# First stage of a two-layer trunk: four receptance buffers, three key-pair buffers, adaLN steps between the mixes with their copies on ScalarE

## The chip, the cores and the metric

The kernel runs as one program on one core of one Trainium2 chip. The metric is the device time of one execution in microseconds (us), of the whole kernel from the first to the last instruction with what lies around it. Engines are named as in the profile: PE is TensorE's matrix multiplication, PEld its weight load, DVE VectorE, ACT ScalarE, POOL GpSimd, SP SyncE (which issues DMAs here). "ACTq" and "SPq" are the queues of ACT and SP on which DMAs are issued.

## What is computed

A trunk of two layers works on 256 latent tokens and 256 context tokens of width 1024, in float32. Each sub-layer is modulated by shift, scale and gate vectors that come from a small product with the layer's adaLN weights. Layer 0 mixes tokens with a bidirectional RWKV-7 recurrence and ends with a SwiGLU; layer 1 has a pooling mixer and a mixture of 8 experts. Cut to what the change touches:

```
mod   = silu(c) @ ada_w[i] + ada_b[i]          # and the same from c_ctx for the context tokens
sh1, sc1, gt1, sh2, sc2, gt2 = split(mod, 6)
h     = x * (1 + sc1) + sh1                    # and hc from ctx
xx    = shifted(h) - h
xr, xw, xk, xv, xa, xg = (h + xx * mu[m] for m in range(6))
r = xr @ w_rkv[0];  k = xk @ w_rkv[1];  v = xv @ w_rkv[2]
d_lora = tanh(xw @ w1) @ w2;   a = sigmoid(a0 + (xa @ a1) @ a2)
kk = k * k_k / |k * k_k|  per head
# wkv7 scan over time in both directions, gate, output product, layer_norm, SwiGLU; then layer 1
```

## The kernel before, in words

The order of instructions on each engine is fixed when the program is built: a scheduler goes through the source and lists the instructions of each engine by when it expects their operands and buffers, so the order on an engine can differ from that of the source. Later, from the recurrence on, a list scheduler of its own with a table of work items decides. Everything named here is the first stage, which comes ahead of the recurrence.

**adaLN steps.** The adaLN product of one layer and one of its six vectors is cut into four steps of `ada_step` (L311). A step loads 1 MB of `ada_w` into one of the raw buffers (L316; `hvr`, `wr` and the two halves of `hvw` for the first eight steps, then `hvr` and `wr`) and issues 16 matmuls (`ada_mm`, L255) into one PSUM bank that all steps share (`ADAB`, pb_68 in the rows of the order). After every fourth step the bank is copied into the tile `ab` (`ada_copy`, L259), two transposes turn it (`ada_turn`, L263), and `ada_put` (L267) adds it to the vectors in `small`. For two of the vectors `ada_store` (L270) writes 1024 single values to `mod_d` in DRAM. The first eight steps give scale and shift, without which no mix can be modulated; eight more stand one behind each pair of the key and of the receptance stage.

**Mixes.** `mixed` (L353) makes the six mixes x + xx * mu before modulation: xk, xw, xa on DVE (L359, 24 instructions of 128x512), xg, xr and xv "beside", scaled on ACT (L356) and added on POOL (L357). Then `modulated` applies scale and shift (`affine`: L388 and L394 on DVE, L391 on ACT) and corrects the edges of the grid (L330).

**Key stage** (L472). Weights come in pairs of output tiles: `wtile` loads 1 MB into a raw buffer, `split_w` splits it into a high part on ACT (L442, two halves) and a low part (L443, the first half on DVE, the second on POOL), each tile takes 24 matmuls (L237) of 128x512. Of each tile the product is copied to `kt` (L480) and squared (L482) on ACT; a matmul sums over heads (L484), DVE takes the reciprocal (L486, L487) and multiplies (L488), and a DMA on ACT's queue writes kt to DRAM (L489). kt has two buffers.

**Receptance stage** (L505). The same for r, with 256 columns; ACT copies the product to `rt` (L514), which has one buffer, and issues its DMA (L515) to `k_d`.

**Into the recurrence.** Then the early pools close. SP reads the first keys back (L1186) and loads the lora weights (L1187, `arena<-in_lr`); ACT issues the next adaLN loads (L702) and splits the lora weights (`lrsh`, L1191; `lrsl` on DVE, L1194); PE multiplies with them (L747), and the recurrence begins.

Of the kernel before, what the change touches and what calls it, by code (L numbers as in the profile page):

```python
# [8 lines left out]
F32 = mybir.dt.float32  # L9
F32R = mybir.dt.float32r  # L10
I32 = mybir.dt.int32
AF = mybir.ActivationFunctionType
# [5 lines left out]
P = 128  # L18
D = 1024
DT = 8  # L20
NT = 512
# [77 lines left out]
class Sched:  # L99


    LAT = {("DVE", "DVE"): 0.06, ("ACT", "ACT"): 0.06, ("POOL", "POOL"): 0.05, ("PE", "PE"): 0.0, ("ACT", "DVE"): 0.12,
           ("PE", "ACT"): 0.14}
# [24 lines left out]
    def order(self):  # L128
# [3 lines left out]
        while cand:  # L132
# [36 lines left out]
            for n in o.next:  # L169
                n.wait -= 1  # L170
                n.ready = max(n.ready, fin + (0.0 if o.nbytes else self.LAT.get((o.eng, n.eng), self.LAT_ELSE)))
                if n.wait == 0:
# [28 lines left out]
def kernel(ctx: ExitStack, tc: tile.TileContext, I: dict, out: bass.AP, dbg=None):  # L201
    nc = tc.nc
# [22 lines left out]
    def C(n, a=0, b=None):  # L225
        o, w = CONST[n]
        return consts[:, o + a:o + (w if b is None else b)]
# [3 lines left out]
    def V(n, dt):  # L231
        return vec[:, n, dt:dt + 1]

    def mm3(ps, a, b, start, stop, pin=None):

        for n, (x, y) in enumerate(((0, 0), (0, 1), (1, 0))):
            i = nc.tensor.matmul(ps, lhsT=a[x], rhs=b[y], start=start and n == 0, stop=stop and n == 2)  # L237
            if pin:
                pin(i)
# [8 lines left out]
    ab = cst.tile([P, 256], F32, name="ab")  # L248
# [4 lines left out]
    def ada_mm(ps, w, k, h):  # L253
        for g in range(2):
            nc.tensor.matmul(ps[64 * h + 32 * g:64 * h + 32 * g + 32, 0:256], lhsT=sct[:, k], rhs=w[:, 256 * g:256 * g + 256],  # L255
                             start=(k == 0), stop=(k == DT - 1))

    def ada_copy(ps):
        nc.vector.tensor_copy(ab, ps[:, 0:256])  # L259

    def ada_turn(pt):
        for j in range(2):
            nc.tensor.transpose(pt[:, P * j:P * j + P], ab[:, P * j:P * j + P], ident)  # L263

    def ada_put(l, w, pt):
        m = mods[l][:, 8 * w:8 * w + 8].rearrange("p (g j) r -> p g j r", g=4)
        nc.vector.tensor_tensor(m, m, pt[:, 0:256].rearrange("p (j g r) -> p g j r", j=2, g=4)[:, :, :, 0:2], op=ALU.add)  # L267

    def ada_store(l, w):
        nc.sync.dma_start(mod_d[l, w // 3].rearrange("(d p) -> p d", p=P), mods[l][:, 8 * w:8 * w + 8, 0])  # L270
# [6 lines left out]
    ADAB = PB[5]  # L277
# [13 lines left out]
    kq = es_e.enter_context(tc.tile_pool(name="kq", bufs=2))  # L291
# [4 lines left out]
    def raw(shape):  # L296

        i = raw_at[0] % (4 if raw_at[0] < 8 else 2)
        raw_at[0] += 1
        return raw_b[i].rearrange("p (a b) -> p a b", a=shape)  # L300

    def xtile(name, dt=F32):
        return xs_p.tile([P, DT, NT], dt, tag="x", name=name)
# [7 lines left out]
    def ada_step():  # L311

        (n, k2) = ada_at
        l, w = todo[n]
        wt = raw(2)
        nc.sync.dma_start(wt, I["ada_w"][l, w, 2 * k2:2 * k2 + 2].rearrange("k p n -> p k n"))  # L316
        for j in range(2):
            for h in range(2):
                ada_mm(ADAB, wt[:, j, 512 * h:512 * h + 512], 2 * k2 + j, h)
        if k2 == 3:  # L320
            ada_copy(ADAB)
            pt = gen()
            ada_turn(pt)
            ada_put(l, w, pt)
            if w % 3 == 2:
                ada_store(l, w)
        ada_at[:] = [n + 1, 0] if k2 == 3 else [n, k2 + 1]
# [25 lines left out]
    def mixed(m, t, sl=slice(0, 512), beside=False):  # L353
        for dt in range(DT):
            if beside:
                nc.scalar.activation(t[:, dt], xx[:, dt, sl], AF.Copy, scale=V(V_MU + m, dt))  # L356
                nc.gpsimd.tensor_tensor(t[:, dt], t[:, dt], xcT[:, dt, sl], op=ALU.add)  # L357
                continue
            nc.vector.scalar_tensor_tensor(t[:, dt], xx[:, dt, sl], V(V_MU + m, dt), xcT[:, dt, sl],  # L359
                                           op0=ALU.mult, op1=ALU.add)  # L360
        return t

    LAT = slice(256, 512)
    xk = mixed(2, xtile("xk"))
    xw = mixed(1, xtile("xw"))
    xa = mixed(4, xtile("xa"))
    xgr = xtile("xgr").rearrange("p a (b c) -> p b a c", b=2)
    xg, xr = mixed(5, xgr[:, 0], LAT, True), mixed(0, xgr[:, 1], LAT, True)
    mixed(3, xv, beside=True)

    for _ in range(8):
        ada_step()
    hvw = hv.tile([P, 4, 4, 256], F32R, tag="hvw", name="hvw1")
    wsp_b = [[hvw[:, 2 * i + j] for j in range(2)] for i in range(2)]
    lr1 = early.tile([P, DT, 384], F32, name="lr1")
# [40 lines left out]
    def modulated(m, x, on=None, then=None, t=None):  # L416
        t = x if t is None else t
        for h in range(2):
            for dt in range(4 * h, 4 * h + 4):
                affine(m, x, t, dt, on)  # L420
            edges(m, t, h)
            for dt in range(4 * h, 4 * h + 4):
                if then:
                    then(t, dt)
# [7 lines left out]
    def lora(xm, o, n):  # L432
        ps = gen()
        for k in range(DT):
            nc.tensor.matmul(ps[:, 0:n], lhsT=lr1[:, k, o:o + P], rhs=xm[:, k], start=(k == 0), stop=(k == DT - 1))
        return ps

    def split_w(w):
        r = []
        for h in range(2):  # L440
            hi, lo = wsp_b[h]
            nc.scalar.activation(hi, w[:, 4 * h:4 * h + 4], AF.Copy)  # L442
            (nc.vector, nc.gpsimd)[h].tensor_tensor(lo, w[:, 4 * h:4 * h + 4], hi, op=ALU.subtract)  # L443
            r.append((hi, lo))
        return r
# [3 lines left out]
    modulated(2, xk, None, split_x(xks, [nc.vector]))  # L449
    modulated(4, xa, nc.scalar)  # L450
    ps = lora(xw, 0, 512)
    tl = kq.tile([P, 2, NT], F32, tag="kt", name="tl")
    nc.scalar.activation(tl[:, 0], ps, AF.Tanh)
    ps = lora(xa, P, 512)
    nc.scalar.activation(tl[:, 1], ps, AF.Copy)
# [11 lines left out]
    def wtile(m, dp):  # L467
        w = raw(DT)
        nc.sync.dma_start(w, I["w_rkv"][m, dp])
        return w  # L470

    for dp in range(4):  # L472
        ws = split_w(wtile(1, dp))
        for j in range(2):
            dt = 2 * dp + j
            ps = gen()
            for k in range(DT):
                mm3(ps, [v[:, k % 4, P * j:P * j + P] for v in ws[k // 4]], [v[:, k] for v in xks], k == 0, k == DT - 1)
            kt = kq.tile([P, 2, NT], F32, name="kt")
            nc.scalar.activation(kt[:, 0], ps, AF.Copy)  # L480
            sq = kq.tile([P, NT], F32, name="sq", bufs=1)
            nc.scalar.activation(sq, ps, AF.Square, scale=V(V_KK, dt))  # L482
            pn = gen()
            nc.tensor.matmul(pn, lhsT=C("bones"), rhs=sq)  # L484
            rec = kq.tile([P, NT], F32, name="rec", bufs=1)
            nc.vector.tensor_scalar(rec, pn, 1e-24, None, op0=ALU.max)  # L486
            nc.vector.reciprocal(rec, rec)  # L487
            nc.vector.scalar_tensor_tensor(kt[:, 1], kt[:, 0], kkh[:, dt:dt + 1], rec, op0=ALU.mult, op1=ALU.mult)  # L488
            nc.scalar.dma_start(k_d[dt, :, 0:1024], kt)  # L489
        ada_step()  # L490
        if dp == 0:
            modulated(5, xg)
            ps = lora(xg, 256, 256)
            nc.scalar.activation(sgg, ps[:, 0:256], AF.Tanh, scale=0.5)
            nc.vector.tensor_scalar(sgg, sgg, 0.5, 0.5, op0=ALU.mult, op1=ALU.add)
            xrt = xtile("xrs", F32R).rearrange("p a (b c) -> p b a c", b=2)
            xrs = [xrt[:, 0], xrt[:, 1]]
            modulated(0, xr, None, split_x(xrs, [nc.gpsimd]))
        if dp == 1:
            xvm = xtile("xvm")  # L500
            modulated(3, xv, None, None, xvm)
            xvs = [xvh, hv.tile([P, DT, NT], F32R, tag="hvl", name="xvl")]
            for dt in range(DT):
                split_x(xvs, [nc.gpsimd, nc.vector])(xvm, dt)
    for dp in range(4):  # L505
        ws = split_w(wtile(0, dp))
        for j in range(2):
            dt = 2 * dp + j
            ps = gen()
            for k in range(DT):  # L510
                mm3(ps[:, 0:256], [v[:, k % 4, P * j:P * j + P] for v in ws[k // 4]], [v[:, k] for v in xrs],
                    k == 0, k == DT - 1)
            rt = kq.tile([P, 256], F32, name="rt", bufs=1)
            nc.scalar.activation(rt, ps[:, 0:256], AF.Copy)  # L514
            nc.scalar.dma_start(k_d[dt, :, 1024:1280], rt)  # L515
        ada_step()
# [807 lines left out]
    p_a, _ = affine(0, 1, 1, None, "pa")  # L1324
# [740 lines left out]
```

## Time and profile before

| | |
|---|---|
| time of the kernel before | 1380.35 us, median of 3 runs (1375.9 to 1383.91) |
| the profiled execution | 1385.43 us, span in the trace 1383.6 us |
| mean granted TensorE clock in it | 0.891 |
| busy: PE, DVE, ACT, POOL | 84%, 66%, 43%, 22% of the span |
| DMA | 287.94 MB, 208 GB/s over the span |

A row of the timeline gives start, busy time, engine, line, operation, output<-inputs with shapes and count, and in brackets how long the engine sat idle before it and what released it. Several like instructions are merged into one row, so its time is from the first start to the last end. A stage's row gives for each engine its busy time and number of instructions.

### The profile page before, as it was taken

To read this page: it belongs to the slowest core of one execution; us is meant where nothing else is said; L and a number is where in the kernel's file an instruction comes from. 1 tells how busy PE (TensorE), PEld (TensorE's weight loads), DVE (VectorE), ACT (ScalarE), POOL (GpSimd) and SP (SyncE) were. 2 spreads that over 40 slices of the span, in tenths; PEclk is the share of its full clock that TensorE was granted. 3 is DMA by queue.
4 is the path that set the end of the run, shared out by engine and by line. 5 is a ranking of instruction groups with operands and counts; after the bars stand their busy time and mean duration, and the time that the engine had idled before them with its cause. 6 is when DMAs were issued, how large, how long until landed. Compare 5 with 4: busy or idle time off the path is not lost. (4 is left out here: it accounts for less than half of the span.)

```text
span 1383.6 us, 26439 instructions
## 1 busy us (share of the span) xinstructions
PE 1165.1 (84%) x10345; PEld 884.2 (64%) x10345; DVE 913.4 (66%) x1792; ACT 596.7 (43%) x1222; POOL 305.8 (22%) x403
## 2 busy tenths in 40 slices
PE   1589658998788787869979999995997999987996
PEld 0256447975556565645569898985785865665673
DVE  7797516868957868234587768675697955723774
ACT  3342116375544563312234444532585844511660
POOL 6341110027530063520162224014000000000000
PEclk8599788998769997788989999997998999999898
DMA  9225545545556374656944554564997844589980
GB/s 363 92 91 196 160 171 172 189 121 163 152 132 172 64 186 117 162 125 192 369 154 146 181 190 155 197 260 178 420 420 287 327 135 164 179 331 414 417 345 32
DMA packets 131546, 287.94 MB, mean 208 GB/s; under 512 B 63536, under 2 KB 90288, under 8 KB 108208
## 3 DMA queue, kind: packets, MB, share of 16 engines
q1 hardware_dynamic: 120000, 249.14, 51.6%
q10 hardware_dynamic: 11376, 36.67, 8.0%
q8 instruction: 90, 1.47, 0.5%
q14 instruction: 80, 0.66, 0.2%
HBM read 273.17 MB, written 12.60 MB: 207 GB/s over the span
## 5 line engine op out<-in xcount | busy, mean ns | idle before, releaser
L1270 DVE TENSOR_TENSOR wl<-arena,wh 128x512 fp32r<-128x512 f32 x266 | 214.9, 833 | 90.2 <-ACT wh L1269 77.6
L1269 ACT ACTIVATE wh<-arena 128x512 fp32r<-128x512 f32 x266 | 162.4, 628 | 134.8 <-PE pb L237 117.8
L237 PE MATMUL pb<-usl,wh 128*128 128x256 f32 x352 | 102.9, 293 | 10.0 <-DVE usl L1419 10.0
L237 PE MATMUL pb<-ush,wl 128*128 128x256 f32 x352 | 102.0, 290 | 1.7 <-DVE wl L1270 1.7
L237 PE MATMUL pb<-ush,wh 128*128 128x256 f32 x352 | 101.4, 291 | 1.8 <-DVE fsg L1437 1.8
L1270 DVE TENSOR_TENSOR wl<-slot,wh 128x512 fp32r<-128x512 f32 x130 | 85.0, 687 | 21.4 <-ACT wh L1269 21.2
L1269 ACT ACTIVATE wh<-slot 128x512 fp32r<-128x512 f32 x130 | 79.3, 629 | 43.5 <-PE pb L237 28.8
L1060 ACT ACTIVATE sv<-pb 64x128 f32<-64x128 f32 x128 | 34.6, 271 | 116.2 <-PE pb L1054 92.6
L237 PEld LDWEIGHTS pb<-usl,wh 128*128 128x128 f32 x352 | 69.9, 199 | 13.7 <-DVE usl L1419 11.0
L1081 DVE TENSOR_TENSOR sv<-pb,wc 64x128 f32<-64x128 f32 x112 | 32.2, 288 | 69.8 <-PE pb L1071 29.2
L237 PE MATMUL pb<-wh,xsh 128*128 128x512 f32 (+1 forms) x192 | 74.2, 392 | 3.1 <-DVE x L1713 3.1
L1643 POOL TENSOR_SCALAR oh<-consts,consts 128x128 f32<-128x128 f32 x14 | 9.8, 710 | 298.3 <-PE pb L237 246.6
L1301 POOL TENSOR_TENSOR arena<-arena,rows 128x2048 f32<-128x2048 f32 x11 | 51.5, 4686 | 108.4 <-DMA arena<-in_ffn_w_dram 108.4
L237 PE MATMUL pb<-wl,xsh 128*128 128x512 f32 (+1 forms) x192 | 75.0, 390 | 0.0
L237 PE MATMUL pb<-wh,xsl 128*128 128x512 f32 (+1 forms) x192 | 72.2, 376 | 0.0
L237 PEld LDWEIGHTS pb<-ush,wl 128*128 128x128 f32 x352 | 69.9, 199 | 3.4 <-DVE wl L1270 2.0
L237 PEld LDWEIGHTS pb<-ush,wh 128*128 128x128 f32 x352 | 69.1, 198 | 4.2 <-DVE fsg L1437 2.0
L930 POOL TENSOR_TENSOR arena<-arena,X 128x126 f32<-128x126 f32 (+22 forms) x124 | 60.1, 485 | 38.5 <-DMA X<-s 29.4
L932 POOL TENSOR_TENSOR arena<-arena 128x126 f32<-128x126 f32 (+22 forms) x124 | 55.3, 446 | 9.7
L1711 PE MATMUL pb<-yf,consts 128*128 128x512 f32 x72 | 42.1, 724 | 17.6 <-issue 14.7
L842 PE MATMUL pb<-arena 64*64 64x192 f32 x512 | 49.0, 339 | 3.2 <-DVE GA L857 1.9
L237 PE MATMUL pb<-hvw,xvh 128*128 128x256 f32 x256 | 47.3, 286 | 1.4 <-DVE hvw L663 1.0
(440 smaller groups left out, 2996.3 us busy)
## 6 DMA issues: line engine op xcount, KB each, us to landing
slot<-in_moe_w_dram SPq DMA_DIRECT2D x62, 1024.0 KB, 13.6
arena<-in_moe_w_dram SPq DMA_DIRECT2D x58, 1024.0 KB, 14.0
arena<-in_ffn_w_dram SPq DMA_DIRECT2D x33, 1024.0 KB, 5.2
arena<-in_ada_w_dram ACTq DMA_DIRECT2D x28, 512.0 KB, 5.2
ada<-in_ada_w_dram ACTq DMA_DIRECT2D x28, 512.0 KB, 4.7
hvr<-in_w_rkv_dram SPq DMA_DIRECT2D x12, 1024.0 KB, 5.3
wr<-in_ada_w_dram SPq DMA_DIRECT2D x10, 1024.0 KB, 8.9
sv<-v_d SPq DMA_DIRECT2D x128, 64.0 KB, 3.6
```

The lines of the kernel that those rows point to most:

```text
L237: i = nc.tensor.matmul(ps, lhsT=a[x], rhs=b[y], start=start and n == 0, stop=stop and n == 2)
L842: nc.tensor.matmul(pb(g)[hs, 192 * j:192 * j + 192], lhsT=kap_b[kap.i][hs, c + j], rhs=kbi_b[kbi.i][hs, c + j])
L930: eng.tensor_tensor(mv, T[:, cs, j:j + 1].to_broadcast([P, nci, nii]), X[:, ii, j].unsqueeze(1).to_broadcast([P, nci, nii]), op=ALU.mult)
L932: eng.tensor_tensor(T[:, cs, ii], T[:, cs, ii], mv, op=ALU.subtract)
L1060: nc.scalar.activation(sv_(si, d, 1)[zd(d)], bank[zd(d), 0:128], AF.Copy, scale=-1.0)
L1081: nc.vector.tensor_tensor(sv_(si + 1, d, 0)[zd(d)].rearrange("p (h x) -> p h x", h=2), bank[zd(d), 128:256].rearrange("p (h x) -> p h x", ...
L1269: nc.scalar.activation(hi, r[:, o:o + PART], AF.Copy)
L1270: nc.vector.tensor_tensor(lo, r[:, o:o + PART], hi, op=ALU.subtract)
L1301: S.behind(nc.gpsimd.tensor_tensor(w, w, gt.unsqueeze(1).to_broadcast(w.shape), op=ALU.mult))
L1643: eng.tensor_scalar(oh[:, t], C2("iota", P * b, P * b + P), posm[:, t, e:e + 1], None, op0=ALU.is_equal)
L1711: nc.tensor.matmul(ps, lhsT=ohT[:, t], rhs=yf[:, 512 * j:512 * j + 512], start=True, stop=True)
```

## The change

It edits the first stage at four places. The adaLN copy can be put on ScalarE, and in the first stage it is (in the recurrence it stays on VectorE). The first eight adaLN steps are written between the mixes, four behind xk and four behind xw, where they stood behind all six. The pool of key pairs gives `kt` (and `tl`, which has the same tag) three buffers for two, and `rt` four for one.

```diff
-    def ada_copy(ps):
-        nc.vector.tensor_copy(ab, ps[:, 0:256])
+    def ada_copy(ps, on=None):
+        if on is nc.scalar:
+            nc.scalar.activation(ab, ps[:, 0:256], AF.Copy)
+        else:
+            nc.vector.tensor_copy(ab, ps[:, 0:256])
...
         if k2 == 3:
-            ada_copy(ADAB)
+            ada_copy(ADAB, nc.scalar)
...
     xk = mixed(2, xtile("xk"))
+    for _ in range(4):
+        ada_step()
     xw = mixed(1, xtile("xw"))
+    for _ in range(4):
+        ada_step()
     xa = mixed(4, xtile("xa"))
...
-    for _ in range(8):
-        ada_step()
...
-    tl = kq.tile([P, 2, NT], F32, tag="kt", name="tl")
+    KT = 3
+    tl = kq.tile([P, 2, NT], F32, tag="kt", name="tl", bufs=KT)
...
-            kt = kq.tile([P, 2, NT], F32, name="kt")
+            kt = kq.tile([P, 2, NT], F32, name="kt", bufs=KT)
...
-            rt = kq.tile([P, 256], F32, name="rt", bufs=1)
+            rt = kq.tile([P, 256], F32, name="rt", bufs=4)
```

Since the scheduler lists each engine's instructions anew, the order on the engines moves too. On ACT, at the front of the program, right behind the mixes (xgr is the tile of xg and xr, hvw the split weights, xkh the high part of xk). Before:

```order
L356 ACTIVATE xgr<-xx,small 128x256 x16
L391 ACTIVATE xw<-xw,small 128x256 x8
L391 ACTIVATE xa<-xa,small 128x256 x8
L442 ACTIVATE hvw_284<-hvr 128x1024 x2
L428 ACTIVATE xkh<-xk 128x512 x8
```

With the change:

```order
L359 ACTIVATE xgr<-xx,small 128x256 x16
L260 ACTIVATE ab<-pb_68 128x256 x2
L448 ACTIVATE hvw_284<-hvr 128x1024 x2
L397 ACTIVATE xw<-xw,small 128x256 x8
L397 ACTIVATE xa<-xa,small 128x256 x8
L434 ACTIVATE xkh<-xk 128x512 x8
```

Both copies of `ab` stand right behind the scaled mixes, and the high halves of the first weight pair stand ahead of the modulation of xw and xa instead of behind it. On DVE at the same place the two copies are gone from between the last mix and the first modulation. Before:

```order
L359 SCALAR_TENSOR_TENSOR xa<-xx,small,xcT 128x512 x8
L259 COPY ab<-pb_68 128x256
L267 TENSOR_TENSOR small<-small,pb_63 128x16
L378 TENSOR_SCALAR small<-small 128x16
L259 COPY ab<-pb_68 128x256
L267 TENSOR_TENSOR small<-small,pb_64 128x16
L381 TENSOR_TENSOR musc<-small 128x48 x2
L388 TENSOR_SCALAR xw<-xw,small 128x256 x8
```

With the change:

```order
L362 SCALAR_TENSOR_TENSOR xa<-xx,small,xcT 128x512 x8
L270 TENSOR_TENSOR small<-small,pb_63 128x16
L384 TENSOR_SCALAR small<-small 128x16
L270 TENSOR_TENSOR small<-small,pb_64 128x16
L387 TENSOR_TENSOR musc<-small 128x48 x2
L394 TENSOR_SCALAR xw<-xw,small 128x256 x8
```

All of DVE's mixes still stand ahead of the first `ada_put`. On PE in the receptance stage (pb_68<-wr is an adaLN step, xrs the two parts of xr, pb_70<-sq and pb_67<-sq the last sums of the key stage), before:

```order
L237 MATMUL pb_65<-xrs,hvw_284 128x256 x10
L255 MATMUL pb_68<-wr,sct 32x256 x8
L484 MATMUL pb_70<-sq,consts 128x512
L237 MATMUL pb_66<-xrs,hvw_284 128x256 x2
L237 MATMUL pb_67<-xrs,hvw_284 128x256 x2
L255 MATMUL pb_68<-wr,sct 32x256 x8
L237 MATMUL pb_66<-xrs,hvw_284 128x256 x22
L237 MATMUL pb_67<-xrs,hvw_284 128x256 x22
L255 MATMUL pb_68<-wr,sct 32x256 x8
L237 MATMUL pb_69<-xrs,hvw_284 128x256 x2
```

With the change:

```order
L491 MATMUL pb_70<-sq,consts 128x512
L237 MATMUL pb_64<-xrs,hvw_284 128x256 x10
L237 MATMUL pb_65<-xrs,hvw_284 128x256 x10
L255 MATMUL pb_68<-wr,sct 32x256 x8
L237 MATMUL pb_66<-xrs,hvw_284 128x256 x2
L237 MATMUL pb_67<-xrs,hvw_284 128x256 x2
L237 MATMUL pb_66<-xrs,hvw_284 128x256 x12
L237 MATMUL pb_67<-xrs,hvw_284 128x256 x12
L237 MATMUL pb_66<-xrs,hvw_284 128x256 x10
L237 MATMUL pb_67<-xrs,hvw_284 128x256 x10
L255 MATMUL pb_68<-wr,sct 32x256 x8
L237 MATMUL pb_69<-xrs,hvw_284 128x256 x2
```

The key stage's last sum no longer stands behind an adaLN step, and the second step has moved from the start of the second pair to its end (the third, likewise, from the start of the third pair to its end). SP's order is the same in both.

## Rows read from the trace of the kernel before

**Rows 1.** Busy time of the engines by stretch of the span: the front's mixes, the first modulation, the lora and first key products. Columns: stretch, its length, busy time and count of PE, PEld, DVE, ACT, POOL, granted PE clock, DMA share, GB/s.

```profile
36.00:46.00 10.00, 0.00 (x0) 0.00 (x0) 10.00 (x11) 0.00 (x0) 7.82 (x7) 0.50 0.00 1
56.00:66.00 10.00, 7.45 (x23) 3.04 (x24) 10.00 (x36) 10.00 (x19) 1.32 (x1) 0.50 0.33 112
66.00:90.00 24.00, 24.00 (x91) 14.24 (x91) 23.94 (x59) 11.05 (x23) 7.37 (x9) 1.00 0.25 88
```

**Rows 2.** The waits between 140 and 212 us, the receptance stage and the way into the recurrence: engine, line, released by, total us, times, longest.

```profile
ACT rt L514 <- DMA k_d<-rt: 19.3, 4, 8.0
...
PE pb L255 <- DMA wr<-in_ada_w_dram: 13.1, 3, 8.0
```

**Rows 3.** The timeline of DVE from the last mix on.

```profile
38.64 7.71 DVE L359 SCALAR_TENSOR_TENSOR xa<-xx,small,xcT 128x512 f32<-128x512 f32 x8
...
53.58 0.42 DVE L259 COPY ab<-pb 128x256 f32<-128x256 f32 x1 [5.73 <-PE pb L255]
54.53 0.17 DVE L267 TENSOR_TENSOR small<-small,pb 128x16 f32<-128x16 f32 x1 [0.53 <-PE pb L263]
54.74 0.33 DVE L381 TENSOR_TENSOR musc<-small 128x48 f32<-128x48 f32 x2
54.98 2.67 DVE L388 TENSOR_SCALAR xw<-xw,small 128x256 f32<-128x256 f32 x8
...
64.96 2.33 DVE L330 TENSOR_TENSOR xa<-xa,musc 128x8 f32<-128x8 f32 x1
```

**Rows 4.** The timeline of PE at the front: the first adaLN group's last step, the first transposes, the end of the second group, the first lora product.

```profile
19.75 1.07 PE L255 MATMUL pb<-hvw,sct 128*32 128x256 f32 x16 [0.97 <-DMA hvw<-in_ada_w_dram]
...
46.74 0.69 PE L263 MATMUL pb<-consts,ab 128*128 128x128 f32 x2 [25.92 <-DVE ab L259]
...
50.78 2.72 PE L255 MATMUL pb<-hvw,sct 128*32 128x256 f32 x32
...
60.48 6.88 PE L435 MATMUL pb<-xw,lr 128*128 128x512 f32 x9 [1.37 <-ACT xa L391]
```

**Rows 5.** The timeline of ACT at the front.

```profile
17.32 6.48 ACT L356 ACTIVATE xgr<-xx,small 128x256 f32<-128x256 f32 x16
...
54.74 4.04 ACT L391 ACTIVATE xw<-xw,small 128x256 f32<-128x256 f32 x8 [30.94 <-DVE small L267]
...
62.61 1.99 ACT L442 ACTIVATE hvw<-hvr 128x1024 fp32r<-128x1024 f32 x2
```

**Rows 6.** The DMA throughput between 10 and 40 us, in 40 slices of 0.75 us: the adaLN loads of the first eight steps.

```profile
DMA  9999999999999998899999999999993000000000
```

**Rows 7.** The timeline of POOL at the front: its last adds, and the first low half of a weight.

```profile
37.01 6.81 POOL L357 TENSOR_TENSOR xgr<-xgr,xcT 128x256 f32<-128x256 f32 x6
64.68 2.58 POOL L443 TENSOR_TENSOR hvw<-hvr,hvw 128x1024 fp32r<-128x1024 f32 x1 [20.86 <-ACT hvw L442]
```

**Rows 8.** The timeline of PE in the key stage, at its only gap there.

```profile
99.70 0.82 PE L237 MATMUL pb<-xkh,hvw 128*128 128x512 f32 x2 [3.77 <-DVE hvw L443]
```

**Rows 9.** The timeline of PE at the end of the receptance stage and behind it.

```profile
188.91 5.53 PE L237 MATMUL pb<-xrs,hvw 128*128 128x256 f32 x44 [0.52 <-DVE hvw L443]
208.21 1.08 PE L255 MATMUL pb<-arena,sct 128*32 128x256 f32 x8 [13.76 <-DMA arena<-in_ada_w_dram]
```

**Rows 10.** The timeline of POOL in the same stretch: the low halves of the last three receptance pairs.

```profile
164.08 2.35 POOL L443 TENSOR_TENSOR hvw<-hvr,hvw 128x1024 fp32r<-128x1024 f32 x1 [18.67 <-ACT hvw L442]
176.96 2.35 POOL L443 TENSOR_TENSOR hvw<-hvr,hvw 128x1024 fp32r<-128x1024 f32 x1 [10.53 <-ACT hvw L442]
188.63 2.48 POOL L443 TENSOR_TENSOR hvw<-hvr,hvw 128x1024 fp32r<-128x1024 f32 x1 [9.32 <-ACT hvw L442]
```

**Rows 11.** The page's DMA issues: line, queue, count, KB each, median us from issue to landing.

```profile
hvr<-in_w_rkv_dram SPq DMA_DIRECT2D x12, 1024.0 KB, 5.3
```

**Rows 12.** The timeline of ACT at the end of the receptance stage.

```profile
196.52 0.38 ACT L514 ACTIVATE rt<-pb 128x256 f32<-128x256 f32 x1 [7.97 <-DMA k_d<-rt]
...
206.94 0.38 ACT L514 ACTIVATE rt<-pb 128x256 f32<-128x256 f32 x1 [5.05 <-DMA k_d<-rt]
...
209.73 0.63 ACT L1191 ACTIVATE lrsh<-arena 128x512 fp32r<-128x512 f32 x1 [2.41 <-PE pb L255]
```

**Rows 13.** SP's queue in that stretch: the second `mod_d` store, the two reads behind it.

```profile
184.70 0.37 SPq L270 DMA_DIRECT2D mod_d<-small  x1
196.02 0.34 SPq L1186 DMA_DIRECT2D arena<-k_d  x1
196.46 0.68 SPq L1187 DMA_DIRECT2D arena<-in_lr_dram  x1
```

**Rows 14.** DMA issues to landing, each from the stretch around its issue (columns as in rows 11): the second `mod_d` store; the receptance write issued at 186.12 us; the lora load; the adaLN load behind the receptance.

```profile
mod_d<-small SPq DMA_DIRECT2D x1, 4.0 KB, 11.2
k_d<-rt ACTq DMA_DIRECT2D x1, 128.0 KB, 10.3
arena<-in_lr_dram SPq DMA_DIRECT2D x1, 256.0 KB, 5.1
arena<-in_ada_w_dram ACTq DMA_DIRECT2D x1, 512.0 KB, 5.8
```

**Rows 15.** The timeline of DVE around the first `mod_d` store: the last step ahead of that store, and the key multiply behind it.

```profile
143.11 0.16 DVE L267 TENSOR_TENSOR small<-small,pb 128x16 f32<-128x16 f32 x1
143.19 2.77 DVE L488 SCALAR_TENSOR_TENSOR kt<-kt,small,rec 128x512 f32<-128x512 f32 x1
```

## The prediction

> **What bounds the kernel now.** I read the busy time by stretch first, then the waits of the stretches in which PE stands still, then each engine's timeline there; the change touches nothing behind the first 210 us, so only what it moves up to the start of the recurrence counts, and everything later is expected to follow by the same amount. Two stretches idle. At the front DVE is busy for all of 36 to 46 us while PE does nothing; from 66 us on PE is busy for 24.00 of 24.00 us [rows 1]. So the front is bound by DVE up to the first modulation, then by PE. In the receptance stage and behind it PE waits for loads: three adaLN loads for 13.1 us together, and ACT waits 19.3 us four times until the one rt buffer has been written out [rows 2]; then PE stands still for 13.76 us until the adaLN load of the recurrence lands [rows 9]. The reader should see there that this load was issued late: it is queued on ACT behind receptance copies that waited [rows 12].
>
> **Term 1, the front.** The data of all eight adaLN steps is there long before it is used: the DMA engines fall idle at about 33 us [rows 6], and the first group's last matmul ends at 20.8 us, yet PE then sits idle for 25.92 us until DVE copies the bank [rows 4]. DVE gets to it only behind the last mix, at 38.64 + 7.71 = 46.35 us [rows 3]. Only then can the second group run in the shared bank, until 53.5 us [rows 4]; its copy waits 5.73 us, and xw is modulated from 54.98 us [rows 3]. ACT meanwhile is done with its mixes at 23.8 us and idle for 30.94 us [rows 5]. With the copies on ACT, the first falls at about 24 us and the second group can end soon after its last data, at about 36 us; both lie under DVE's mixes. What stays behind the last mix is two additions of 0.17, one scalar step of the same size and 0.33 for musc [rows 3], about 0.7 us in all: xw begins at 47.0 instead of 54.98 us, **-8.0 us**. The two copies themselves (0.4 us each) leave DVE and lie in ACT's idle time. That DVE's order puts both additions behind all mixes costs nothing, since the mixes have to be made anyway.
>
> Two things bear on it. The weight's high halves now run on ACT at about 36 us, not at 62.61 [rows 5], so POOL's low half can follow its last add, which ends at 43.8 us, instead of running at 64.68 us [rows 7]. An instruction of DVE that fell beside it took 2.33 us for 8 columns [rows 3]; a stall like that now falls on the last mixes, up to 2.3 us lost, and the old one at 64.96 goes. The edge fixes of xw stand two modulations later in DVE's order, some 0.65 us. On the other side the 3.77 us for which PE waited on DVE's low half at 99.70 [rows 8] should shrink or go, as DVE starts ahead of PE by more. From there to the end of the key stage PE has no gap, so what the front gains arrives at its end: between 6.0 (both losses, with the old stall's relief not reaching PE, -8.0 + 2.3 + 0.65 = -5.1, and a part of the 3.77) and 9.5 us. I take 8.
>
> The third kt buffer by itself I cost at nothing: ACT's waits for the DMA of kt in the key stage did not hold PE, which has no gap there but that one. If PE's cover were gone it would be worth a few us more.
>
> **Term 2, receptance and the way into the recurrence**, in the times of before (the 8 us are taken off afterwards). Each pair is a chain: the raw buffer is loaded, 5.3 us [rows 11]; ACT makes the high halves, 2.0 us [rows 5]; POOL makes its low half, 2.4 us; then the raw buffer is free for the next pair. POOL's second pair ends at 164.08 + 2.35 = 166.4, its third at 179.3, its fourth at 191.1 us [rows 10]: 12.9 and 11.8 us apart where the chain itself needs 9.8 (0.1 between). The difference was DVE's low half, which stood behind a late last sum of the key stage (a sum that PE's order had behind an adaLN step), and ACT, which made high halves only behind an rt copy that waited. In the changed order the sum comes early and rt has four buffers. So the third ends at 176.2 and the fourth at 186.0. PE's last product ended at 188.91 + 5.53 = 194.44 [rows 9], 3.3 us behind POOL; now 189.3 us.
>
> From there to `lrsh` took 15.3 us (209.73 us). The reason stands in [rows 12]: the last rt copies wait 7.97 and 5.05 us for writes, with the adaLN loads behind them. Without those waits: two copies and issues of 0.4 each, the load of 5.8 us [rows 14], a step of PE of 1.1 us [rows 9], and 0.4 us to ACT, together 8.2 us, gives 197.5 us. But `lrsh` also needs the lora load, which SP issues behind a read that waits for the second `mod_d` store: 184.70 + 11.2 = 195.9, the read at 196.02, the load at 196.46 and 5.1 us [rows 13, 14]. The store now comes behind an adaLN step at the end of the third pair and its copy on ACT, at about 182.0: landed 193.2, lora weights at 198.9 us. The later of the two decides, 198.9 against 209.7: -10.8 us.
>
> What could be late: the first `mod_d` store. Its `ada_put` now stands behind the key multiply that followed it and took 2.77 us [rows 15], so it is issued some 2.8 us later, and loads issued behind a store of that kind were slow: the receptance write behind the second one took 10.3 us [rows 14] and landed with it. If all loads of the stage move with it, every time above is 2.8 later, -8.0 us. If none does, -10.8. No row tells which; I take the middle, **-9.5 us**, and keep both ends.
>
> The Trainium skill (DMA: Bandwidth & Descriptors, section "Queues, rings and completion order") states that a completion is a strongly ordered write, which lands only after every earlier write of the same DMA engine, whichever queue it came from. By that rule the loads behind the first store signal with it at the earliest, and the sum would be the smaller gain of 8.0 us here. The trace agrees as far as the receptance write's 10.3 us goes.
>
> **Sum.** -8 and -9.5 make -17.5 us. The profiled execution took 1385.43 us, 5 us above the median of 1380.35; against its own time that is 1368, against the median about **1363 us**. The gain is of a size that doesn't depend on which of the two one takes.
>
> **The rivals.**
> *Only one of the two terms arrives* (-8 to -9.5, about 1371 us). For it: the waits for adaLN loads, 13.1 us [rows 2], stay, and the order now puts all eight high parts of xv on ACT, and four low ones on POOL, ahead of the second key pair's second half, up to 6 us in which PE could wait in a stage that had no gap. Against: that pair's low halves were made well ahead, and the gain at the front gives DVE and POOL more lead, not less.
> *No change*, about 1380 us: the waits only move on. The rt copies would no longer wait, but the loads behind them would, until the stores land; and the front's gain would meet a load of the key stage that comes no sooner. Against: the weight loads of the key stage are issued when PE and POOL free their buffers, which come earlier too, and DMA stood idle at the front.
> *Slower*, about 1390 us. PE now has its second adaLN group before 36 us and then nothing until about 52, and its granted clock is at the lower level (0.50) in 36 to 46 as in 56 to 66 us, before it reaches 1.00 [rows 1]. If it stayed at the lower level through the key stage instead of rising, products there would take twice as long: 54 us at the lower level hold 27 us of work at the full one and lose 27, and 27 less the 17.5 gained gives 1390. It decides from about 35 us longer at the lower level, where the 17.5 are used up. Against: before, PE had been idle for 25.92 us as well [rows 4], and the clock rose within a few us of steady products.
>
> **How the numbers follow.** The forecast, both terms, has 0.68: each mechanism stands in a row, and every later row depends on what moves. One term alone 0.20, no change 0.08, slower 0.04. The low end of the range takes the best of both (-9.5 and -10.8, with the third kt buffer and the last waits worth a few us more), 1355; the high end takes in one term alone with a loss in it, 1374. Beyond it lie no change and slower, and a little of the rest. A measurement can tell about 0.5%, 6.9 us, from no change; of the one-term case I count 0.03 as within that. So faster 0.85, same 0.11, slower 0.04.
>
> **What would show it.** Right: both copies of `ab` on ACT ahead of 40 us, xw's modulation beginning by 48 us, the first lora product by 55 us, the end of the key stage's products 6 to 9.5 us earlier; rt copies without a wait for a write; POOL's last low halves some 10 us apart; `lrsh` near 192 us. Wrong: a gap of PE in the key stage, an `ada_put` that comes after the mixes by more than 1 us, a granted clock of 0.50 beyond 70 us, or `lrsh` later than 200 us. And if the recurrence begins 17 us earlier and the whole is not that much shorter, a later stage has absorbed it.

## The result and the profile after

The changed kernel took 1366.78 us in the median of 6 runs (1360.65 to 1370.17), the kernel before 1380.35 us in the median of five beside it (a sixth execution, of 2176.24 us, lies far off and is not counted). The comparison of the runs gives a ratio of **0.9906, 95% interval 0.9881 to 0.993**, that is 13.0 us less (9.7 to 16.4). The forecast was 1363 us, 17.5 us less. The profiled execution took 1360.65 us with a span of 1358.9 us; it is 6 us below the median, and that of before was 5 above it, so the two spans (24.7 us apart) overstate the change. What can be compared is the first stage, up to `lrsh`: 209.73 us before, 193.40 now. From the adaLN copy on, the lines of the changed kernel's code stand 3 to 7 higher.

The front, the answers to [rows 3, 4, 5, 7]. The timeline of DVE:

```profile
38.73 9.81 DVE L362 SCALAR_TENSOR_TENSOR xa<-xx,small,xcT 128x512 f32<-128x512 f32 x8
48.46 0.16 DVE L270 TENSOR_TENSOR small<-small,pb 128x16 f32<-128x16 f32 x1
...
49.18 2.67 DVE L394 TENSOR_SCALAR xw<-xw,small 128x256 f32<-128x256 f32 x8
```

The timeline of ACT, of POOL and of PE there:

```profile
23.75 0.36 ACT L260 ACTIVATE ab<-pb 128x256 f32<-128x256 f32 x1
36.91 0.38 ACT L260 ACTIVATE ab<-pb 128x256 f32<-128x256 f32 x1 [12.79 <-PE pb L255]
```

```profile
43.88 2.78 POOL L449 TENSOR_TENSOR hvw<-hvr,hvw 128x1024 fp32r<-128x1024 f32 x1
```

```profile
55.28 8.61 PE L441 MATMUL pb<-xw,lr 128*128 128x512 f32 x16 [13.50 <-DVE xw L333]
...
89.71 0.73 PE L237 MATMUL pb<-xkh,hvw 128*128 128x512 f32 x2 [1.02 <-DVE hvw L449]
...
102.70 0.50 PE L237 MATMUL pb<-xkh,hvw 128*128 128x512 f32 x1 [1.05 <-ACT hvw L448]
108.21 0.73 PE L237 MATMUL pb<-xkh,hvw 128*128 128x512 f32 x2 [1.72 <-DVE hvw L449]
...
134.37 0.39 PE L237 MATMUL pb<-xkh,hvw 128*128 128x512 f32 x1
```

The copies fall at 23.75 and 36.91 us, in ACT's idle time, as forecast. xw begins at 49.18 instead of 54.98 us: 5.8 us gained, not 8.0. Of the missing 2.2 us, 2.1 stand in the first row: the eight mixes of xa took 9.81 instead of 7.71 us [rows 3], and POOL's low half (43.88 to 46.66 us) lies beside them. The key stage's last product ends at 134.76 us instead of 141.67, 6.9 us earlier.

The receptance stage and the way on, the answers to [rows 9, 10, 12, 13]. POOL's low halves, PE, ACT and SP's queue:

```profile
156.99 2.47 POOL L449 TENSOR_TENSOR hvw<-hvr,hvw 128x1024 fp32r<-128x1024 f32 x1 [18.85 <-ACT hvw L448]
167.26 2.48 POOL L449 TENSOR_TENSOR hvw<-hvr,hvw 128x1024 fp32r<-128x1024 f32 x1 [7.80 <-ACT hvw L448]
177.02 2.45 POOL L449 TENSOR_TENSOR hvw<-hvr,hvw 128x1024 fp32r<-128x1024 f32 x1 [7.28 <-ACT hvw L448]
```

```profile
151.19 1.93 PE L255 MATMUL pb<-wr,sct 128*32 128x256 f32 x16 [6.81 <-DMA wr<-in_ada_w_dram]
156.02 8.27 PE L237 MATMUL pb<-xrs,hvw 128*128 128x256 f32 x48 [2.90 <-ACT hvw L448]
...
177.30 7.03 PE L237 MATMUL pb<-xrs,hvw 128*128 128x256 f32 x44 [0.52 <-DVE hvw L449]
190.99 1.08 PE L255 MATMUL pb<-arena,sct 128*32 128x256 f32 x8 [6.66 <-DMA arena<-in_ada_w_dram]
```

```profile
183.17 0.38 ACT L521 ACTIVATE rt<-pb 128x256 f32<-128x256 f32 x1 [6.23 <-PE pb L237]
...
184.37 0.38 ACT L521 ACTIVATE rt<-pb 128x256 f32<-128x256 f32 x1 [0.81 <-PE pb L237]
...
193.40 0.63 ACT L1198 ACTIVATE lrsh<-arena 128x512 fp32r<-128x512 f32 x1 [8.65 <-DMA arena<-in_lr_dram]
```

```profile
135.69 0.37 SPq L273 DMA_DIRECT2D mod_d<-small  x1
...
175.25 0.37 SPq L273 DMA_DIRECT2D mod_d<-small  x1
184.36 0.34 SPq L1193 DMA_DIRECT2D arena<-k_d  x1
184.75 0.68 SPq L1194 DMA_DIRECT2D arena<-in_lr_dram  x1
```

The low halves end 10.3 and 9.7 us apart (9.8 forecast); rt copies wait for PE, no longer for a write; PE's gap before the recurrence is 6.66 us for 13.76. From the key stage's end to `lrsh` it is 58.6 us for 68.1. What PE still waits for is the load behind the first `mod_d` store (6.81 us) and the weights after it (2.90), and `lrsh` waits 8.65 us for the lora load.

### The profile page after: what moved, and what is told of

Read it like the earlier page. It is cut to its first block, busy times and chain, and to the rows that moved or that the text cites. A ratio compares the mean times of both kernels' runs of the same rounds, so it can differ in the third digit from the quotient of the medians.

```text
span 1358.9 us, 26431 instructions
## 1 busy us (share of the span) xinstructions
PE 1163.4 (86%) x10345; PEld 883.6 (65%) x10345; DVE 915.1 (67%) x1788; ACT 596.9 (44%) x1226; POOL 307.6 (23%) x403
## 4 chain that ended last, share of the span: by engine, by line
PE 46%; DVE 6%; DMA 2%; issue 2%; ACT 1%; POOL 0%; DVEq 0%; ACTq 0%; POOLq 0%
PE pb L237 26%; PE pb L1745 4%; PE pb L1718 2%; PE pb L1659 2%; DMA slot<-in_moe_w_dram 2%; PE pb L1237 2%; PE pb L1780 2%; PE pb L1763 1%; DVE usl L1426 1%; PE pb L1794 1%; PE pb L1061 1%; ACT wh L1276 1%; DVE wl L1277 1%; PE pb L1078 0%; PE pb L1075 0%
```

## The experiments

All were timed against the kernel before on the same chip, but for e8_before, which is the kernel before itself, profiled once more. "lrsh" is the start of `lrsh` in the profiled execution, "key end" the end of the last key product.

| run | what it has | key end | lrsh | ratio, 95% interval |
|---|---|---|---|---|
| before, and e8_before | | 141.67, 141.74 | 209.73, 208.45 | 1 |
| e1_copy | ACT copies | 141.07 | 206.64 | 1.0032 (1.0012 to 1.0052) |
| e2_rt | rt 4 | 140.90 | 204.58 | 0.9972 (0.9953 to 0.999) |
| e3_kt | kt 3 | 140.38 | 205.79 | 0.9987 (0.997 to 1.0005) |
| e4_ktrt | kt 3, rt 4 | 140.88 | 201.22 | 0.9983 (0.9965 to 1.0001) |
| e5_copy_kt | ACT copies, kt 3 | 134.73 | 196.29 | 0.9949 (0.9929 to 0.9968) |
| e6_copy_rt | ACT copies, rt 4 | 140.95 | 209.48 | 1.0031 (1.0 to 1.0062) |
| e7_noplace | all but the steps' place | 134.80 | 194.21 | 0.9909 (0.9879 to 0.9939) |
| the change | all | 134.76 | 193.40 | 0.9906 (0.9881 to 0.993) |
| e9_late | all, stores later | 134.86 | 183.08 | 0.983 (0.9801 to 0.986) |
| e10_nopool | all, first low half off POOL | 132.15 | 191.49 | 0.9911 (0.9882 to 0.994) |
| e11_both | both of these | 132.81 | 181.28 | 0.9858 (0.9829 to 0.9886) |

**The copies alone.** The edit, from the change:

```diff
-    KT = 3
+    KT = 2
...
-            rt = kq.tile([P, 256], F32, name="rt", bufs=4)
+            rt = kq.tile([P, 256], F32, name="rt", bufs=1)
... (and the eight steps behind the mixes again)
```

> Of the change only the adaLN copies on ScalarE; the steps stay behind the mixes in the source, kt has two buffers and rt one. The order on every engine is the one that the placed steps give too. Theory (two terms that add): the front's term alone. xw is modulated from about 49 us instead of 54.98, the first lora product begins at about 55 instead of 60.5 us, and lrsh stands at about 202 us instead of 209.7, since ACT still waits for rt's writes: time -7 to -9 us, ratio 0.994. Rival (the front does it all, buffers are worth nothing): lrsh at about 193.5 us, ratio 0.990. Rival (the front's lead is absorbed by the key stage's loads): lrsh at 209 us, ratio 1.000.

Measured: the front gains what it does in the whole change (xw at 49.33, lora at 55.44 us), but the key stage ends at 141.07 us, 0.6 us earlier than before, `lrsh` comes 2.5 us earlier than the mean of the two profiles of before (209.1) instead of 7 to 9, and the kernel is slower by 0.32%. No forecast holds: the front's gain is made and then lost within the key stage. The timeline of ACT in that kernel, and of PE:

```profile
109.32 0.33 ACTq L494 DMA_DIRECT2D k_d<-kt  x1
116.71 0.60 ACT L485 ACTIVATE kt<-pb 128x512 f32<-128x512 f32 x1 [10.61 <-DMA k_d<-kt]
...
117.21 0.68 ACT L487 ACTIVATE sq<-pb,small 128x512 f32<-128x512 f32 x1
```

```profile
117.94 2.08 PE L489 MATMUL pb<-sq,consts 128*128 128x512 f32 x2 [5.39 <-ACT sq L487]
```

ACT holds the fourth kt copy until the write issued at 109.32 us lets its buffer go, after 10.61 us of waiting; the square stands behind the copy, and the sum on PE behind the square, in a place of PE's order where nothing else could run: 5.39 us. The kernel before has a wait of that length too, at its third copy, and no gap on PE; in the changed kernel the fourth copy waits for no write:

```profile
111.63 0.60 ACT L480 ACTIVATE kt<-pb 128x512 f32<-128x512 f32 x1 [10.24 <-DMA k_d<-kt]
112.99 1.12 PE L484 MATMUL pb<-sq,consts 128*128 128x512 f32 x2
```

```profile
109.28 0.60 ACT L487 ACTIVATE kt<-pb 128x512 f32<-128x512 f32 x1 [4.63 <-DVE kt L495]
```

Two things make the wait an open one. PE gets to the sum earlier, by the front's lead. And the write that ends the wait is slower. DMA issues to landing between 108 and 110 us, first of before, then with the copies alone:

```profile
k_d<-kt ACTq DMA_DIRECT2D x1, 512.0 KB, 2.6
```

```profile
hvr<-in_w_rkv_dram SPq DMA_DIRECT2D x1, 1024.0 KB, 7.7
k_d<-kt ACTq DMA_DIRECT2D x1, 512.0 KB, 7.3
```

With the lead, two loads of 1 MB (an adaLN step at 106.92 and a weight at 108.77 us) are issued just ahead of the write, and it takes 7.3 us; before, none lies beside it and it takes 2.6. Landed as fast as that, it would have let the copy go 4.7 us sooner, nearly the whole gap (an estimate from these rows). The gap costs more than its length. The stretch from 118 to 124 us, columns as in [rows 1], first of before, then with the copies alone:

```profile
118.00:124.00 6.00, 6.00 (x26) 4.62 (x25) 4.22 (x4) 0.47 (x2) 0.00 (x0) 1.00 0.89 337
```

```profile
118.00:124.00 6.00, 6.00 (x13) 4.05 (x14) 3.91 (x2) 1.79 (x3) 0.00 (x0) 0.52 0.15 61
```

Behind the gap the granted clock is 0.52, and half as many products start; the changed kernel has 1.00 there. At 0.52 the 6 us hold 2.9 us less work (an estimate). Gap and clock make 8.3 us; the changed kernel has 2.0 us more in small gaps of PE (3.8 against 1.8), which leaves 6.3, the difference of the two key ends.

**The buffers alone.**

> Of the change only the four rt buffers; the order on the engines stays that of before, but for one adaLN step that moves from the middle to the end of the third receptance pair. Theory: ACT no longer waits 7.97 and 5 us for writes of rt and the adaLN loads of the recurrence are issued some 12 us earlier, but the second mod_d store comes about 2 us later and the lora load behind it, so lrsh stands at about 205 us: -4 to -5 us, ratio 0.997. Rival (loads behind the store land with it, nothing to gain): lrsh at 209 to 212 us, ratio 1.000 or above.

> Of the change only the three kt buffers. Theory: it changes PE's order (the key stage's last sum ahead of the adaLN step) and with it DVE's low half of the second receptance pair; the third pair's load is issued some 2 us earlier, and rt's waits then take most of it back: lrsh at about 207 to 209 us, -1 to -3 us, ratio 0.999. Rival (the kt waits of 10.2 and 9.1 us on ACT were worth their length in the key stage): lrsh at 200 us or earlier, ratio 0.993.

> Three kt and four rt buffers, the adaLN copies on VectorE as before. Theory (two terms that add): the second term alone, -8.0 to -10.8 us: lrsh at about 199 to 202 us, ratio 0.993; together with the run of the copies alone it makes the whole change's 16 us at lrsh. Rival (front does it all): lrsh at 209 us, ratio 1.000. If the sum of rt alone and kt alone falls short of this run by more than 3 us, the two buffers work only together.

Measured: with four rt buffers `lrsh` comes 4.5 us before the mean of before (209.1), as forecast, and the kernel is 3.9 us faster. Three kt buffers alone are worth 3.3 us at `lrsh`, a little more than forecast, and within noise in time. Both together give 7.9 us at `lrsh`, the sum of the two, where the second term said 8.0 to 10.8; in time only 0.17%, with an interval that touches no change. So at `lrsh` the second term arrived nearly whole without the first; in the time it can't be seen. The forecast that this run and the copies alone together make the whole change failed: 7.9 and 2.5 us are 10.4 at `lrsh`, where the change has 15.3. The parts do not simply add.

**Which buffer lets the front's gain through.**

> Copies on ScalarE and three kt buffers; rt has one buffer, the steps stay behind the mixes in the source. Theory (the third kt buffer lets the front's gain through the key stage, since with two PE waited 5.39 us on a sum behind a kt copy that waited 10.61 us for a write): the key stage's last product ends at 134 to 135 us as in the whole change, instead of 140.7 with the copies alone; rt's waits then cost some 5 us, lrsh at 198 to 201 us, ratio 0.993 to 0.995. Rival (the four rt buffers let it through): key stage's end at 140 us, lrsh at 204 to 207 us, ratio 1.000 or above.

> Copies on ScalarE and four rt buffers; kt has two buffers, the steps stay behind the mixes in the source. Theory (third kt buffer needed): the key stage ends at 140 to 141 us as with the copies alone, lrsh at 202 to 204 us, ratio 0.999 to 1.001. Rival (rt needed): key stage's end at 135 us, lrsh at 194 us, ratio 0.991.

Measured: the third kt buffer does. With it the key stage ends at 134.73 us, with four rt buffers instead at 140.95, and PE stands still for 6.82 us behind a kt copy that waited 12.04 for a write of 8.7 us. Each has a partner that differs by kt's buffer alone: e5_copy_kt ends the key stage 6.3 us before e1_copy, and e7_noplace 6.2 us before e6_copy_rt. The runs make up every combination of the three parts, so the buffer's worth can be read with and without the copies. Without them it is 3.3 and 3.4 us at `lrsh` (before to e3_kt, e2_rt to e4_ktrt); with them 10.4 and 15.3 us (e1_copy to e5_copy_kt, e6_copy_rt to e7_noplace), and 0.8% and 1.2% in time. Without a third kt buffer the copies bring nothing in time: 1.0032 alone, and 1.0031 with rt's buffers, where the interval reaches 1.0. In the second of these `lrsh` stands over 5 us later than forecast: the lora load is issued 2.6 us behind the second `mod_d` store and `lrsh` waits 15.66 us for it. SP's queue and ACT there:

```profile
191.25 0.37 SPq L273 DMA_DIRECT2D mod_d<-small  x1
193.82 0.68 SPq L1192 DMA_DIRECT2D arena<-in_lr_dram  x1
```

```profile
209.48 0.63 ACT L1196 ACTIVATE lrsh<-arena 128x512 fp32r<-128x512 f32 x1 [15.66 <-DMA arena<-in_lr_dram]
```

The lora load landed 15.6 us after its issue where it took 5.1 before [rows 14], and 6.7 us behind the store, which took 11.5. Not all of it is the store's price: without a store ahead, in e9_late below, `lrsh` still waits 7.72 us for the load. In the kernel before the price lies elsewhere, in the wait ahead of the read [rows 13].

**The place of the steps, and before again.**

> The whole change, but the first eight adaLN steps stand behind the mixes in the source as before. Theory (the scheduler places the steps by when their data comes, so their place in the source does nothing): the order on every engine is that of the whole change, lrsh at 192 to 195 us, ratio 0.988 to 0.993. Rival (the place matters): lrsh at 198 us or later.

> The kernel before, a second look, to see how far one execution's time at lrsh and its time behind lrsh move by themselves. Theory (the stages up to lrsh are steady, what varies lies behind it): lrsh at 208 to 210 us, and the rest of the span within 1165 to 1175 us. Rival (the first stage varies as much): lrsh at 206 us or below.

Measured: without the new places the order on every engine is the same, and so are `lrsh` (194.21 us) and the ratio. That part of the change does nothing: the scheduler had put the steps' matmuls where their data comes in any case. The second profile of before has `lrsh` at 208.45 us, 1.3 us from the first; from there, the recurrence up to its last product took 459.0 us in the first profile and 452.5 us in the second. So in these two executions of one program the first stage is steadier than the recurrence.

**The stores, and the rest of the front.** The edits, on the change:

```diff
             if w % 3 == 2:
-                ada_store(l, w)
+                late.append((l, w))
...
             nc.sync.dma_start(lr2_b[R["lr2"].i], I["lr2"][:, :, P * u:P * u + P])
+            if u == 2:
+                for lw in late:
+                    ada_store(*lw)
```

```diff
-            (nc.vector, nc.gpsimd)[h].tensor_tensor(lo, w[:, 4 * h:4 * h + 4], hi, op=ALU.subtract)
+            lo_on[h].tensor_tensor(lo, w[:, 4 * h:4 * h + 4], hi, op=ALU.subtract)
...
-        ws = split_w(wtile(1, dp))
+        ws = split_w(wtile(1, dp), (nc.vector, nc.gpsimd) if dp else (nc.vector, nc.vector))
```

> The whole change, with the first stage's two mod_d stores issued later: both behind the third unit's key and lora loads in the recurrence (some 30 us behind lrsh), where only SP's order differs. Theory (loads issued behind a store of that kind land with it at the earliest): the adaLN load of the first receptance step and the weight load land some 6 us sooner, PE's wait of 6.81 us on it goes to about 1, the lora load lands in 5 instead of 8.65 us, and lrsh stands at 184 to 187 us instead of 193.4; ratio to before 0.983 to 0.987. Rival (the loads there take their time by their own bytes): PE still waits 5 us or more, lrsh at 191 to 194 us, ratio 0.990. A second rival (the recurrence pays for the stores instead): lrsh early, ratio 0.990 all the same.

> The whole change, with both low halves of the first weight pair on VectorE, so that POOL does not work on its low half (43.9 to 46.7 us) beside the last mixes. Theory (the front's missing 2 us are VectorE held beside POOL): the mixes end at 46.4 instead of 48.5 us and xw is modulated from 47.1 us; the first lora product begins at about 53.3; by the end of the key stage 1 to 2 us of it are left, ratio 0.989 to 0.991. Rival (the mixes are slow by themselves): xw still from 49 us.

> The whole change with both of the other two edits: late mod_d stores and the first pair's low halves on VectorE. Theory: the two add, lrsh at 183 to 186 us, ratio 0.982 to 0.986. Rival: no better than the late stores alone, since the receptance loads set the end.

Measured: with the stores out of the way PE's wait for the adaLN load of the first receptance step is gone, and `lrsh` comes 10.3 us earlier than in the change. DMA issues to landing in the stretch from 134 to 140 us, first of the change, then of the late stores (KB each, us to landing):

```profile
wr<-in_ada_w_dram SPq DMA_DIRECT2D x1, 1024.0 KB, 13.0
...
mod_d<-small SPq DMA_DIRECT2D x1, 4.0 KB, 11.2
```

```profile
wr<-in_ada_w_dram SPq DMA_DIRECT2D x1, 1024.0 KB, 5.0
```

The same load behind the store took 13.0 us and without it 5.0. In the change it is issued at 138.10 us, with the late stores at 138.20. The GB/s that the DMA engines moved from 134 to 154 us, in 40 slices of 0.5 us, first of the change, then of the late stores:

```profile
GB/s 0 0 0 0 0 426 361 247 22 25 9 0 0 0 0 57 49 41 41 33 41 33 33 33 57 41 49 33 66 319 426 475 410 377 401 492 418 426 410 401
```

```profile
GB/s 0 0 0 33 0 360 385 262 25 16 106 49 352 426 426 410 451 401 475 442 377 393 434 401 344 330 43 209 344 360 385 369 197 107 115 131 82 246 295 426
```

Behind the store the loads moved at 33 to 66 GB/s from 141.5 to 148.5 us, and over 300 only then; without it they moved at over 350 from 140 us. PE and ACT with the late stores:

```profile
146.79 0.74 PE L237 MATMUL pb<-xrs,hvw 128*128 128x256 f32 x4 [1.31 <-ACT hvw L449]
...
180.65 1.08 PE L255 MATMUL pb<-arena,sct 128*32 128x256 f32 x8 [5.71 <-DMA arena<-in_ada_w_dram]
```

```profile
183.08 0.63 ACT L1202 ACTIVATE lrsh<-arena 128x512 fp32r<-128x512 f32 x1 [7.72 <-DMA arena<-in_lr_dram]
```

The first theory holds and neither rival does: 1355.18 us against 1379.34, 0.983 (0.9801 to 0.986). Of the 10.3 us at `lrsh`, 9.4 are there at the end of the last receptance product (174.94 instead of 184.33 us), so it is the first store that cost nearly all of it. One part of the theory was wrong: `lrsh` still waits 7.72 us for the lora load without a store ahead, beside three other loads and the read of the keys.

With both low halves on VectorE the mixes are as fast as before. The timeline of DVE in e10_nopool:

```profile
38.61 7.72 DVE L362 SCALAR_TENSOR_TENSOR xa<-xx,small,xcT 128x512 f32<-128x512 f32 x8
...
46.97 2.67 DVE L394 TENSOR_SCALAR xw<-xw,small 128x256 f32<-128x256 f32 x8
```

xw begins at 46.97 us, the 47.0 of the forecast, and the key stage and `lrsh` come 2.6 and 1.9 us earlier than in the change. Together with the late stores the two add at `lrsh`, 12.1 us. The time doesn't show it, neither alone (0.9911) nor together (0.9858; its interval overlaps that of the late stores alone).

"As fast as before" is not undisturbed. Three single mixes of xa in the changed kernel, DVE's timeline:

```profile
38.73 1.21 DVE L362 SCALAR_TENSOR_TENSOR xa<-xx,small,xcT 128x512 f32<-128x512 f32 x1
44.39 2.82 DVE L362 SCALAR_TENSOR_TENSOR xa<-xx,small,xcT 128x512 f32<-128x512 f32 x1
47.80 0.74 DVE L362 SCALAR_TENSOR_TENSOR xa<-xx,small,xcT 128x512 f32<-128x512 f32 x1
```

The first lies beside POOL's additions of xgr, the second beside the low half, the third with POOL idle. So POOL's additions slow DVE's mixes as well, by about 0.5 us each; the front is bound by DVE in part because POOL works beside it. No run moves the additions.

## Why the prediction held, and where not

**The front, term 1.** The mechanism was right: the copies at 24 and 36 us were forecast and stand at 23.75 and 36.91, and of what lay between the last mix and xw 0.6 us is left. The size was 5.8 us for 8.0, and the bound named for it, POOL's low half beside the last mixes, is the cause: 2.1 us of DVE, gone when the half is moved. At the key stage's end the gain is 6.9 us, more than at xw; part of that is the clock, with 0.70 granted from 60 to 70 us before and at least 0.98 in the change.

Two of the signs named were missed by little (xw at 49.18 for 48, the first lora product at 55.28 for 55 us).

**The third kt buffer was mis-sized.** This is the step that failed. I costed it at nothing since PE had no gap in the key stage, and added that it would be worth a few us if PE's cover were gone. It was gone, by the lead that term 1 gives, which also set the kt write beside two loads: with two buffers 0.6 us of the front's gain is left at the end of the key stage, with three 6.9. The buffer carries 6.3 us there, and the two parts are one term. The whole change's 6.9 lies in the forecast's 6.0 to 9.5 because the change brings both, which is luck as far as the buffer goes.

**Term 2** was forecast between -8.0 and -10.8 us from the key stage's end to `lrsh`, -9.5 taken; it measured 68.1 and 66.7 us before, 58.6 and 59.4 (the run without the new places) after: -7.3 to -9.4. The chain of loads and weight halves was right (10.3 and 9.7 us a pair), the working behind it only half. The fear that the first store would come 2.8 us later was void: it is issued 0.9 us behind the last key product, where before it was 1.6, as the key multiply ahead of it no longer lies beside POOL and takes 0.74 instead of 2.77 us [rows 15]. And the chain from the second store to the lora load, on which I let `lrsh` hang (198.9 us), is not there in the changed kernel. SP's waits, first of before between 140 and 212 us, then of the change between 170 and 205 us:

```profile
SPq L1186 <- DMA mod_d<-small: 10.8, 1, 10.8
```

```profile
SPq L1193 <- PE pb L237: 8.7, 1, 8.7
```

The read that stands ahead of the lora load waited for the store before, and now waits for PE's last product alone. In the traces the loads and writes of this stretch signal their landing on eight semaphores in turn (100 and 102 to 108). Before, the read and the store have the same one (105), and the read was issued at 196.02 us, just behind the store's landing at 195.9; in the changed kernel they have 104 and 107. That this sharing is what made the read wait is the likely cause and was not tested. So the lora load was issued at 184.75 us, just behind PE's end at 184.33, and what takes the wait's place is its landing: 8.65 us for 5.1, with two adaLN loads beside it. It ends on the forecast time (193.4 against 198.9 less the 6.9 that the key stage gained, 192.0) for a reason that is partly another, so the time there was right by luck in part.

**The page's rule.** The Trainium skill (DMA: Bandwidth & Descriptors, section "Queues, rings and completion order") says that a completion lands only after every earlier write of the same DMA engine. The runs agree that far: the store issued at 135.69 us landed at 146.9, the load issued behind it at 151.1. But the load did not land with the store; it came 4.2 us later, and what was late was the moving of its bytes, as the GB/s above show. The rule bounds the landing from below and does not give the size; why the bytes move slowly behind such a store is not shown. Moving the stores was worth more than the rt buffers.

**The rivals.** "Only one of the two terms arrives" did not happen for the whole change; apart, the buffers bring the second term at `lrsh` (7.9 us) and the copies little (2.5). The waits it expected in the key stage, which are also a sign named for being wrong, come to three gaps of PE of 1.02, 1.05 and 1.72 us, together as long as the one of 3.77 us that before had there [rows 8]. "No change" fell. "Slower" did not come by the clock. The stretches of the changed kernel, columns as in [rows 1]:

```profile
46.00:52.00 6.00, 0.00 (x0) 0.00 (x0) 5.93 (x17) 3.06 (x7) 0.67 (x1) 0.50 0.03 12
52.00:58.00 6.00, 2.72 (x3) 1.18 (x4) 6.00 (x26) 5.65 (x12) 0.00 (x0) 0.50 0.00 0
58.00:64.00 6.00, 6.00 (x18) 2.58 (x20) 6.00 (x20) 3.71 (x8) 0.00 (x0) 0.98 0.00 0
```

PE idles from 41.8 to 55.28 us at the lower level (0.50) and has 0.98 in the stretch from 58 us on, earlier than before (0.50 until 66 us). The sign "0.50 beyond 70 us" did come, in the receptance stage (0.50 from 151 to 157 us), but before has it there too (0.50 from 160 to 166).

**Open.** At `lrsh` the change gains 15.3 us (193.4 and 194.2 against 209.7 and 208.4), in time 13.0 (9.7 to 16.4). The interval allows that nothing is lost behind `lrsh`. But all eleven kernels of the table gain less in time than at `lrsh`, by 0.6 to 8.2 us, so some loss behind it is likely. The copies alone show it most plainly: `lrsh` comes 2.5 us earlier and the kernel takes 4.4 us more (1.7 to 7.2). Every instruction behind the first stage has the same order in these kernels. From `lrsh` to the last product of the recurrence the trace shows 452.5 and 459.0 us for before, 455.4 for the change, 462.3 with the copies alone; one profile of each does not tell a lasting difference from one that comes and goes. The mean granted clock of the copies alone is 0.892 over its 12 runs, against 0.896 over 35 of before on the same chip; whether that is cause or consequence is not shown. Why the copies alone are slower than before in time is not settled.

## What to carry to other kernels

A wait that holds no one was priced here at the cover it had; when another part of the same change used up that cover, and moved loads beside the write that ended it, the wait opened. So the parts must be costed together: copies on an idle engine brought nothing (0.3% slower) until a third buffer stood behind them. Where a stage waits for loads, look at what was issued just ahead of them: two stores of 4 KB in single values cost 10.3 us at `lrsh`, where the whole change gained 15.3, and the time went from 0.9906 to 0.983 of before when they were moved.

## What the runs showed of the hardware

A 4 KB store of 1024 single values took 11.2 us to land; a 1 MB load issued 2.4 us behind it took 13.0 instead of 5.0 us, most of it at 33 to 66 GB/s. A 512 KB write took 2.6 us with no load beside it and 7.3 us with two 1 MB loads issued up to 2.4 us ahead. One VectorE instruction of 128x512 with two tensor inputs took 0.74 us alone, 1.21 beside GpSimd's additions of 128x256, and 2.82 beside one GpSimd subtraction of 128x1024 (2.78 us). Behind a gap of TensorE of 5.39 us the granted clock was 0.52 for the next 6 us.
